# Latent attention by one written order of three engines, the next pair's expansions inside it, and o_B projected by token halves

## The chip, the cores and the metric

The kernel runs on one core of one Trainium2 chip. Its metric is the device time of one launch in microseconds (us). Four compute engines work beside each other: TensorE (PE) multiplies, VectorE (DVE) and ScalarE (ACT) work element by element, GpSimd (POOL) does small things and starts some transfers; SyncE (SP) starts the rest. The kernel lets PE write into eight banks of 512 columns of PSUM, which ACT and DVE read.

## What is computed

One encoder layer on 1024 prompt tokens and on 32 sample tokens with a past of 512. Two attention branches read one projection of the normalised input; the change is in branch A and in the projection of branch B's output.

```python
q = (rms_norm(q_lat, g_q_lat) @ w_uq).reshape(B, T, H_A, NOPE + ROPE)   # 8 heads, 64 + 32
k_nope, v_a = expand_latent(c_kv, w_uk, w_uv)                          # (c_kv @ w_uk), (c_kv @ w_uv)
s = (einsum('bqhd,bshd->bhqs', q_nope, k_nope)
     + einsum('bqhr,bsr->bhqs', q_rope, k_rope)) * MLA_SCALE
mask = (kpos[None, :] // CHUNK) <= (qpos[:, None] // CHUNK)            # CHUNK = 64
o_A = einsum('bhqs,bshd->bqhd', softmax(where(mask, s, NEG)), v_a)
merged = sigmoid(gate A) * (o_A @ w_proj_a) + sigmoid(gate B) * (o_B @ w_proj_b)
```

o_B comes from stick-breaking attention, which ran before. After `merged` come w_out, a residual, and a convolutional feed-forward block, none of them touched.

## The kernel before

A product is kept near fp32 by splitting each operand into a rounded high half and a low rest: `hi` (L60) is an ACT copy, `lo` (L63) a DVE subtraction, and `mm3` (L66) issues three products, high x high, high x low, low x high. Weights come through `wload` (L73; SP, two raw buffers "wr") and are split into "wh" and "wl", two buffers each.

The stages follow one another: `stage_h`, `stage_sb` (stick-breaking attention), `stage_lat` (latents), `stage_mla` (L1008), `stage_merge`, `stage_up`, `stage_down`. Within a stage a compile-time scheduler orders each engine's instructions by their priority and a cost model, except where a `manual_schedule` block holds: there PE, ACT and DVE keep the written order. `stage_sb` has such a block for each of its four head pairs: `ORDER` (L491) is a list of short words, `sb_attend` (L513) turns each into its instructions, and the words f, G, D, W, w call `gates` (L778), an independent projection whose products fill PE.

`stage_mla` before has none. For each of four head pairs p (L1020):
- it loads and splits w_uq and w_uk of the pair; `queries` (L1070) makes two heads' queries (18 mm3 of 352 columns, a multiplication by the rotary table on DVE at L1075, then hi and lo), `keys` (L1062) writes both heads' keys (4 mm3 of 512 columns) into the one pair of key buffers; for p 0 and 2 `values` (L1041) makes the values of four heads;
- for the sample, `mla_sample_expand` (L1174) makes keys and values of four heads from the cached latent, in column blocks of 272 and 272, (at p = 0 and 3), and `mla_sample` (L1197) attends (at p = 1 and 3);
- `attend` (L656) runs each head over u, the blocks of 256 query rows (0 to 3 for the first head, 3 to 0 for the second). For each of the 2 row tiles of 128 it makes scores (`score`, L1097: high x high, high x low, a mask product of 64 columns at L1104 for the diagonal, low x high) in one or two PSUM banks "s" (three of them), then `mla_weights` (L627): maximum on DVE (L633), exp with a row sum on ACT (L641), reciprocal on DVE, and the scaling on DVE (L651) or ACT (L653). Then pairs of 128-blocks are transposed on PE (L680) into a bank "tr" (two), split by hi and lo into PTh and PTl (or the two "ptd" tiles on the diagonal), and multiplied with the values (L693) into the one bank "pv", which is added up by ACT (L697) and DVE (L698);
- `proj_b` (L1233) projects one quarter of the tokens (264) of o_B: four loads and splits, then for each of 8 row tiles of w_proj_b a load, a split of 512 columns, 4 mm3, an ACT copy (L1250) and a store on POOL's queue. Its 384 products are independent of the attention, and the scheduler puts them where PE would wait.

After the four pairs the loop reads back the outputs of pairs 0 to 2, splits them and begins the products of w_proj_a with them (L1128 to 1146); the last pair's output is split directly.

Of the kernel before, what the change touches and what calls it, by code (L numbers as in the profile page):

```python
# [8 lines left out]
F32 = mybir.dt.float32  # L9
# [8 lines left out]
P = 128  # L18
D = 1024
KT = 8  # L20
# [17 lines left out]
UT = 1060  # L38


class K:
# [471 lines left out]
    def sb_attend(self, score, V, out, fill):  # L513
        nc = self.nc
        act, vec = nc.scalar.activation, nc.vector
        tiles, banks, seen, turned, pv, res = {}, {}, {}, {}, {}, {}
        for x in self.ORDER:
# [6 lines left out]
            if k in "SaelxckdE":  # L524
# [33 lines left out]
                continue  # L558
            n, jb = x[0], int(x[2:] or 0)
# [9 lines left out]
            elif k == "V":  # L569
                if jb == u:  # L570
                    pv[n] = self.bank("pv")
                self.values(h, u, jb, pv[n], V, turned.pop(x)[1:])
            else:
                r, q = slice(64 * h, 64 * h + 64), slice(64 - 64 * h, 128 - 64 * h)
                if k == "o":
                    res[n] = self.tl(self.At, [P, 256], F32, "o")
                    nc.scalar.copy(res[n][r], pv[n][q, :256])
                else:
                    vec.tensor_tensor(res[n][r], pv[n][r, :256], res[n][r], ALU.add)
                    out(res[n], r, slice(u * 256, u * 256 + 256))  # L580

# [44 lines left out]

    def mla_weights(self, pieces, w):  # L627
# [27 lines left out]

    def attend(self, h, score, weights, V, out, order=(0, 1, 2, 3)):  # L656

        nc = self.nc
        for u in order:
            at = []  # L660
            for i in (2 * u, 2 * u + 1):
                w = (i + 1) * P
                np_ = 1 if w <= 512 else 2
                n = w // np_
                pieces = []
                for j in reversed(range(np_)):
                    ps = self.tl(self.ps, [P, 512], F32, "s")
                    score(h, ps, i, j * n, max(n, 256), j == np_ - 1)
                    pieces.append((ps, j * n, n))
                at.append(weights(pieces, w))  # L670
            pv = self.bank("pv")
            for jb in range(2 * u, -1, -2):
                diag = jb == 2 * u
                tr = self.bank("tr")
                c0 = P if diag else 0
                for s in range(2):
                    b = jb + 1 - s
                    for q in range(2):
                        if b <= 2 * u + q:
                            nc.tensor.transpose(tr[:, (2 * s + q) * P : (2 * s + q + 1) * P],  # L680
                                                at[q][:, b * P : b * P + P], self.idt)
                if diag:
                    ph, pl = self.PTd[self.ptd_i % len(self.PTd)]
                    self.ptd_i += 1
                else:
                    ph = self.tl(self.At, [P, 512], F32R, "PTh")
                    pl = self.tl(self.At, [P, 512], F32R, "PTl")
                self.hi(ph[:, c0:], tr[:, c0:])
                self.lo(pl[:, c0:], tr[:, c0:], ph[:, c0:])
                for s in range(2):  # L690
                    b = jb + 1 - s
                    for j, x in enumerate((ph, pl)):
                        nc.tensor.matmul(pv[:, :256], V[:, b, h], x[:, s * 256 : s * 256 + 256],  # L693
                                         start=(diag and s == 0 and j == 0), stop=(jb == 0 and s == 1 and j == 1))
            o = self.tl(self.At, [P, 256], F32, "o")
            r, q = slice(64 * h, 64 * h + 64), slice(64 - 64 * h, 128 - 64 * h)
            nc.scalar.copy(o[r], pv[q, :256])  # L697
            nc.vector.tensor_tensor(o[r], pv[r, :256], o[r], ALU.add)  # L698
            out(o, r, slice(u * 256, u * 256 + 256))
# [198 lines left out]
    def stage_lat(self):  # L898
# [10 lines left out]
        self.QZm = L.tile([P, 4, 64], F32, name="QZm")  # L909
# [98 lines left out]
    def stage_mla(self):  # L1008
# [11 lines left out]
        for p in range(4):  # L1020
# [5 lines left out]
            h = self.tl(self.W, [P, 1024], F32R, "wh")  # L1026
            l = self.tl(self.W, [P, 1024], F32R, "wl")
            rq = raw[:, 0:576].rearrange("p (k h c) -> p k h c", k=3, h=2)
            hq, lq = (x[:, 0:768].rearrange("p (k h c) -> p k h c", k=3, h=2) for x in (h, l))
            for d0, s0, n in ((0, 0, 96), (96, 80, 16), (112, 64, 16)):  # L1030
                d, x = (slice(None),) * 3 + (slice(d0, d0 + n),), rq[:, :, :, s0 : s0 + n]
                self.hi(hq[d], x)
                self.lo(lq[d], x, hq[d])
            self.hi(h[:, 768:1024], raw[:, 576:832])
            self.lo(l[:, 768:1024], raw[:, 576:832], h[:, 768:1024])
            hk, lk = (x[:, 768:1024].rearrange("p (k c) -> p k c", k=2) for x in (h, l))
            KH, KL = ([x[(2 * p + e) % NK] for e in range(2)] for x in (KHs, KLs))
            gt = "mm" if p else "mm s s"
            QH, QL = [], []

            def values():  # L1041
                hf = p // 2
                raw = self.wload([(0, 512, a["w_uv"][0, :, hf * 256 : hf * 256 + 256]
                                   .rearrange("(k p) c -> p k c", p=P), 2)])
                h, l = self.wsplit(raw, 512)
                Vs = [self.tl(O, [P, 2 * T], F32R, "V")[:, : 16 * P].rearrange("r (t h d) -> r t h d", t=8, h=2)
                      for _ in range(2)]
                for t in range(0, 8, 2):
                    ps = self.bank(gt.split()[t // 2 % len(gt.split())])
                    for j in range(2):  # L1050
                        tk = slice((t + j) * P, (t + j + 1) * P)
                        for k in range(2):
                            self.mm3(ps[:, j * 256 : j * 256 + 256], self.CPh[k][:, tk], self.CPl[k][:, tk],
                                     h[:, k * 256 : k * 256 + 256], l[:, k * 256 : k * 256 + 256], k == 0, k == 1)
                    pv = ps.rearrange("r (j q h d) -> r j q h d", j=2, q=2, h=2)
                    for q in range(2):
                        self.hi(Vs[q][:, t : t + 2, :, 0:64], pv[:, :, q])
                        self.lo(Vs[q][:, t : t + 2, :, 64:128], pv[:, :, q], Vs[q][:, t : t + 2, :, 0:64])

                return Vs  # L1060

            def keys():  # L1062
                for c0, n, ps in self.mtile(hk, lk, self.CPh, self.CPl, ((0, 512), (512, 512)), 2, gt):
                    c = slice(c0, c0 + n)
                    for e in range(2):
                        r = slice(64 * e, 64 * e + 64)
                        self.hi(KH[e][0:64, c], ps[r, :n])
                        self.lo(KL[e][0:64, c], ps[r, :n], KH[e][0:64, c])

            def queries():  # L1070
# [998 lines left out]
```

## Time and profile before

| | |
|---|---|
| median of three runs | 1746.15 us (1742.15 to 1746.4) |
| the profiled execution | 1746.93 us, span 1745.2 us |
| granted TensorE clock, mean | 0.994 |
| ACT busy share of the span | 58% |
| HBM read and written | 174.25 MB and 51.25 MB |

A row of a timeline gives start, duration, engine, line, operation, output<-input and form. A row of a group gives line, engine, operation, output<-input, partitions x elements, the count, then busy time and mean ns of one, then the idle time before them and what ended it. "PE s L1105" is an instruction of PE that writes tile s at line 1105. PE's matmuls overlap in its pipeline and their ends are modelled. A stage's window starts at the first instruction named for it.

### The profile page before, as it was taken

How to read it: one execution, taken by the hardware profiler on the slowest of the kernel's cores; microseconds unless marked ns; L12 is line 12 of the kernel's file. 1: busy time of each engine (PE TensorE's matmuls, PEld its weight loads, DVE VectorE, ACT ScalarE, POOL GpSimd, SP SyncE). 2: the span in 40 equal slices, each digit the busy share in tenths (PEclk: the TensorE clock that was granted, in tenths of full speed). 3: DMA queues.
4: the chain of work that ended last, by engine and by line, in shares of the span. 5: the costliest groups of instructions: out<-in, count | busy, mean ns of one | idle time of the engine just before them, and what ended most of it. 6: DMA issues, size and time to landing. Idle time of an engine off the chain costs nothing. (4 is left out here: it accounts for less than half of the span.)

```text
span 1745.2 us, 29960 instructions
## 1 busy us (share of the span) xinstructions
PE 1701.0 (97%) x11546; PEld 1544.6 (89%) x11546; DVE 1259.0 (72%) x2133; ACT 1007.4 (58%) x1976; POOL 273.6 (16%) x519
## 2 busy tenths in 40 slices
PE   6999999999999999999999999999999999999998
PEld 3899999999989988888888779999999999977886
DVE  4596594693873678788686678887787787788456
ACT  4595594783872666867775267544444444544442
POOL 2211111111110001111000031212111111110013
PEclk8999999999999999999999999999999999999999
DMA  9343333333341222313346531434423323597743
GB/s 323 92 124 101 106 119 84 114 105 90 111 123 53 68 58 78 93 54 102 103 172 200 183 127 49 150 105 131 135 92 128 128 91 128 205 332 247 243 148 118
DMA packets 181695, 227.46 MB, mean 130 GB/s; under 512 B 13349, under 2 KB 129776, under 8 KB 181552
## 3 DMA queue, kind: packets, MB, share of 16 engines
q1 hardware_dynamic: 166048, 182.10, 33.2%
q0 software_dynamic: 15280, 43.35, 7.0%
q8 instruction: 91, 1.49, 0.3%
q14 instruction: 52, 0.43, 0.1%
q10 hardware_dynamic: 224, 0.09, 0.0%
HBM read 174.25 MB, written 51.25 MB: 129 GB/s over the span
## 5 line engine op out<-in xcount | busy, mean ns | idle before, releaser
L61 ACT ACTIVATE wh<-wr 128x1024 fp32r<-128x1024 f32 (+6 forms) x181 | 146.0, 813 | 259.4 <-PE s L1523 78.8
L64 DVE TENSOR_TENSOR wl<-wr,wh 128x1024 fp32r<-128x1024 f32 (+6 forms) x181 | 164.6, 916 | 145.3 <-ACT wh L61 141.9
L68 PE MATMUL mm<-hh,wh 128*128 128x352 f32 x696 | 232.1, 333 | 2.8 <-ACT nat L811 2.8
L69 PE MATMUL mm<-hl,wh 128*128 128x352 f32 x696 | 227.1, 326 | 0.3 <-DVE hl L288 0.3
L70 PE MATMUL mm<-hh,wl 128*128 128x352 f32 x696 | 226.0, 325 | 0.0
L68 PEld LDWEIGHTS mm<-hh,wh 128*128 128x128 f32 x696 | 131.5, 189 | 10.5 <-ACT nat L811 4.8
L69 PEld LDWEIGHTS mm<-hl,wh 128*128 128x128 f32 x696 | 131.5, 189 | 3.5 <-DVE hl L288 1.9
L70 PEld LDWEIGHTS mm<-hh,wl 128*128 128x128 f32 x696 | 131.6, 189 | 0.4 <-issue 0.4
L1524 PE MATMUL s<-T,wl 128*128 128x256 f32 (+1 forms) x328 | 93.6, 285 | 0.0
L1523 PE MATMUL s<-T,wh 128*128 128x256 f32 (+1 forms) x328 | 93.4, 285 | 0.0
L1522 PE MATMUL s<-T,wh 128*128 128x256 f32 (+1 forms) x328 | 93.3, 284 | 0.0
L1663 DVE SCALAR_TENSOR_TENSOR u<-u,c,u 128x1058 f32<-128x1058 f32 x68 | 87.0, 1317 | 2.0 <-ACT u L1660 0.7
L1522 PE MATMUL tr<-T,wh 128*128 128x272 f32 (+1 forms) x272 | 77.7, 286 | 0.0
L1524 PE MATMUL tr<-T,wl 128*128 128x272 f32 (+1 forms) x272 | 77.6, 285 | 0.0
L1523 PE MATMUL tr<-T,wh 128*128 128x272 f32 (+1 forms) x272 | 77.3, 284 | 0.0
L64 DVE TENSOR_TENSOR wl<-S,wh 128x1024 fp32r<-128x1024 f32 x40 | 48.9, 1223 | 34.8 <-ACT wh L61 34.8
L1524 PE MATMUL mm<-T,wl 128*128 128x256 f32 (+1 forms) x256 | 72.9, 286 | 0.3 <-DVE wl L64 0.2
L1522 PE MATMUL mm<-T,wh 128*128 128x256 f32 (+1 forms) x256 | 73.0, 285 | 0.0
L1523 PE MATMUL mm<-T,wh 128*128 128x272 f32 (+1 forms) x256 | 72.7, 284 | 0.0
L64 DVE TENSOR_TENSOR PTl<-tr,PTh 128x512 fp32r<-128x512 f32 x96 | 64.0, 683 | 8.5 <-ACT PTh L61 8.2
L1653 POOL COPY c<-u 128x2 f32<-128x2 f32 x44 | 26.7, 608 | 259.1 <-DVE u L1599 224.0
L61 ACT ACTIVATE wh<-S 128x1024 fp32r<-128x1024 f32 x40 | 42.4, 1060 | 35.0 <-PE s L1523 13.3
(674 smaller groups left out, 5618.9 us busy)
## 6 DMA issues: line engine op xcount, KB each, us to landing
wr<-in_w_ada_dram SPq DMA_DIRECT2D x48, 512.0 KB, 4.6
wr<-in_w_up_dram SPq DMA_DIRECT2D x44, 512.0 KB, 4.1
dr<-in_w_down_dram SPq DMA_DIRECT2D x43, 512.0 KB, 5.3
wr<-in_w_in_dram SPq DMA_DIRECT2D x33, 512.0 KB, 4.7
wr<-gdn SPq DMA_DIRECT2D x30, 512.0 KB, 4.9
gdn<-u POOLq DMA_DIRECT2D x23, 512.0 KB, 5.0
gd<-nat POOLq DMA_DIRECT2D x48, 176.0 KB, 2.2
t<-gd SPq DMA_DIRECT2D x16, 528.0 KB, 4.5
```

What stands on the lines that cost most here:

```text
L61: self.nc.scalar.activation(out, in_, AF.Identity, scale=scale)
L64: return self.nc.vector.tensor_tensor(out, full, hi.bitcast(F32), ALU.subtract)
L68: m(ps, lh, rh, start=start, stop=False)
L69: m(ps, lh, rl, start=False, stop=False)
L70: self.pe = m(ps, ll, rh, start=False, stop=stop).ins
L1522: m(ps[:, :n], w[0][:, k], x[0][:, k, c], start=first and k == 0, stop=False, skip_group_check=True)
L1523: m(ps[:, :n], w[0][:, k], x[1][:, k, c], start=False, stop=False, skip_group_check=True)
L1524: i = m(ps[:, :n], w[1][:, k], x[0][:, k, c], start=False, stop=k == 3, skip_group_check=True)
L1653: nc.gpsimd.tensor_copy(self.CV[:, 0:2, cc], u[:, 1024:1026])
L1663: nc.vector.scalar_tensor_tensor(y, u[:, w : w + YW], self.cvT[:, w, cc : cc + 1], y, ALU.mult, ALU.add)
```

## The change

`attend` goes. Two written orders come, ORDER_A for pairs 0 to 2 and ORDER_L for the last, and `mla_attend` turns their words into instructions inside a `manual_schedule` block, as `sb_attend` does. The words T, h, v, V, o, p (transposes, hi, lo, products with values, sums) are now one function, `sums`, for both attentions. Attention's words are S scores, M maximum, m its join over two banks, E exp, s sum's join, R reciprocal, C scaling on DVE, c on ACT.

The other words fill:
- f, G, U, W, w, O are `proj_b`: one mm3, a store, a load, a high half, a low half, the operands. It now goes by halves of the tokens (528), each in two column blocks of 264, and w_proj_b's eight row tiles come in six loads of one or two.
- I, i, x, X, y, H, L, z, J, j, Z are the next pair's expansion: split of its weights, queries of head 0 (x), keys (y), queries of head 1 (z), and their evictions. They are in ORDER_A only; pair 0's own run ahead of the loop.
- Y is a step of the sample's second attention, q and r the split of an output; these are in ORDER_L only.

Between the blocks, without a written order: for p = 1 `mla_sample_keys` and the sample's first expansion, for p = 2 the keys again, the values of heads 4 to 7, the sample's first attention, the second expansion, and o_B's second operands. The sample's cached and new latents are kept in separate tiles, so its expansions have column blocks of 512 and 32. The wh and wl buffers are taken once as the two sets AB, shared by all of this. The second head's rotary key rows are copied from the first's by two POOL transfers in place of a second split.

```diff
+PARTS = ((0, 0, 96), (96, 80, 16), (112, 64, 16))
...
+    ORDER_A = """
+        S0.0 S0.1 S1.0 W f M0.0 f M0.1 M1.0 f E0.0 f E0.1 w f E1.0 S1.1 G R0.0 R0.1 R1.0 c0.0 S2.0a C0.1 c1.0
+        M1.1 S2.0b M2.0a T0.0 E1.1 f M2.0b h0.0 f R1.1 m2.0 C1.1 E2.0a f v0.0 E2.0b S2.1a G s2.0 S2.1b R2.0
...
+        T4.2 X c5.0 S5.1b h4.3 S6.0 h4.2 M5.1b x v4.3 x v4.2 T4.1 m5.1 M6.0 E5.1a V4.3 h4.1 V4.2 E5.1b x v4.1
+        E6.0 T4.0 s5.1 X f R5.1 R6.0 W V4.1 C5.1 S6.1 G w h4.0 T5.2 c6.0 v4.0 S7.0 h5.2 x M6.1 T5.1 v5.2 E6.1
+        V4.0 M7.0 h5.1 x R6.1 C6.1 o4 T5.0 v5.1 E7.0 x h5.0 p4 S7.1 R7.0 X c7.0 y v5.0 J V5.2 M7.1 V5.1 Z E7.1 j
+        V5.0 T6.1 o5 T6.0 h6.1 R7.1 p5 y C7.1 h6.0 v6.1 z v6.0 H z H L V6.1 V6.0 L T7.0 o6 z h7.0 p6 z X z v7.0
+        z y X V7.0 y o7 p7 z H z H L z L X Z J j
+    """.split()
+
+    ORDER_L = """
+        S0.0 S0.1 S1.0 W f M0.0 f M0.1 M1.0 f E0.0 f E0.1 w S1.1 E1.0 G S2.0a R0.0 R0.1 R1.0 c0.0 M1.1 c1.0
...
+        h3.3 s4.0 R4.0 h3.2 v3.3 c4.0 f v3.2 T3.1 Y f h3.1 S4.1a G v3.1 V3.3 M4.1a V3.2 V3.1 T3.0 S4.1b h3.0
+        S5.0a v3.0 f M4.1b f V3.0 M5.0a f m4.1 o3 f E4.1a p3 G q S5.0b E4.1b r M5.0b S5.1a s4.1 m5.0 R4.1 E5.0a
+        C4.1 E5.0b S5.1b M5.1a T4.3 s5.0 M5.1b T4.2 h4.3 R5.0 S6.0 m5.1 c5.0 v4.3 h4.2 M6.0 T4.1 E5.1a V4.3 v4.2
+        h4.1 E5.1b V4.2 v4.1 E6.0 T4.0 s5.1 R5.1 V4.1 R6.0 C5.1 h4.0 S6.1 c6.0 v4.0 T5.2 M6.1 T5.1 h5.2 V4.0
+        E6.1 v5.2 S7.0 o4 T5.0 R6.1 h5.1 M7.0 p4 S7.1 h5.0 C6.1 V5.2 v5.1 q E7.0 v5.0 T6.1 V5.1 r h6.1 V5.0 R7.0
+        M7.1 c7.0 v6.1 T6.0 E7.1 o5 R7.1 h6.0 C7.1 p5 v6.0 q V6.1 r V6.0 T7.0 o6 h7.0 p6 v7.0 q r V7.0 o7 p7 q r
+    """.split()
...
+        AB = [[self.tl(self.W, [P, 1024], F32R, g) for g in ("wh", "wl")] for _ in range(2)]
...
+        proj = self.proj_b(M, AB)
+        steps, QH, QL = expansion(0, "mm s s")
+        raw = load_values(0)
+        steps["I"]()
+        steps["i"]()
+        for _ in range(2):
+            for k in "yyHHLL":
+                steps[k]()
+        Vs = values(0, raw, "mm s s")
+        proj["O"]()
+
+        self.hi(KHs[0][64:128], self.KRp[64:128])
+        self.lo(KLs[0][64:128], self.KRp[64:128], KHs[0][64:128])
+        for x in (KHs, KLs):
+            nc.gpsimd.dma_start(x[1][64:128], x[0][64:128])
+        for k in "xxxXxxxXxxxXJjZ":
+            steps[k]()
+        for k in "zzzXzzzXzzzXJjZ":
+            steps[k]()
+        for k in "UUWwU":
+            proj[k]()
+
+        for p in range(4):
+            if p == 1:
+                expanded = self.mla_sample_expand(M, raw, AB[1], *self.mla_sample_keys(M))
+            if p == 2:
+                cn = self.mla_sample_keys(M)
+                Vs = values(1, raw, "mm")
+                for _ in self.mla_sample(0, QZ, QR, *expanded):
+                    pass
+                proj["U"]()
+                expanded = self.mla_sample_expand(M, raw_s, AB[1], *cn)
+                proj["O"]()
+            if p in (1, 2):
+                for k in "UWwU":
+                    proj[k]()
...
+            with self.tc.manual_schedule(engines={E.PE, E.Activation, E.DVE}):
+                self.mla_attend(self.ORDER_L if p == 3 else self.ORDER_A, score, Vs[p % 2], out, fill)
...
+    def proj_b(self, M, AB):
...
+        HB = HC // 2
+        TILES = ((0, 1), (1, 2), (3, 1), (4, 1), (5, 2), (7, 1))
...
+        def operands():
+            h = done[0] // 6
+            ob[:] = [self.tl(M, [P, 4, HC], F32R, g) for g in ("ObH", "ObL")]
+            for k in range(4):
+                f = self.tl(self.At, [P, BIG], F32, "big")[:, :HC]
+                nc.sync.dma_start(f, self.obd[k][:, h * HC : h * HC + HC])
+                self.hi(ob[0][:, k], f)
+                self.lo(ob[1][:, k], f, ob[0][:, k])
```

446 lines of the change are left out of this document (277 added, 169 removed).

## Prediction

> **What bounds the kernel now.** I read the page's totals first.
>
> ```profile
> span 1745.2 us, 29960 instructions
> PE 1701.0 (97%) x11546; PEld 1544.6 (89%) x11546; DVE 1259.0 (72%) x2133; ACT 1007.4 (58%) x1976; POOL 273.6 (16%) x519
> ```
>
> TensorE is the bound, and by this row nearly without a gap, so a new order could win little. But the ends of matmuls are modelled: one that waits inside the array's pipeline still counts as busy. So I next read starts, in the timeline of PE, in fed stretches:
>
> ```profile
> 644.25 0.28 PE L70 MATMUL mm<-ObH,wl 128*128 128x264 f32 x1
> 644.37 0.28 PE L68 MATMUL mm<-ObH,wh 128*128 128x264 f32 x1
> 644.68 0.47 PE L1100 MATMUL s<-KH,QH 128*128 128x448 f32 x1
> ...
> 645.39 0.40 PE L1100 MATMUL s<-KH,QH 128*128 128x512 f32 x1
> 645.62 0.39 PE L1101 MATMUL s<-KL,QH 128*128 128x512 f32 x1
> 645.86 0.20 PE L1104 MATMUL s<-c,c 128*128 128x64 bf16 x1
> 645.89 0.48 PE L1105 MATMUL s<-KH,QL 128*128 128x512 f32 x1
> ...
> 881.99 0.32 PE L68 MATMUL mm<-KH,wh 128*128 128x352 f32 x1
> 882.15 0.32 PE L69 MATMUL mm<-KL,wh 128*128 128x352 f32 x1
> 882.30 0.32 PE L70 MATMUL mm<-KH,wl 128*128 128x352 f32 x1
> 883.40 0.50 PE L1100 MATMUL s<-KH,QH 128*128 128x512 f32 x1 [0.78 <-ACT A L641]
> ...
> 885.80 0.98 PE L680 MATMUL tr<-c,A 128*128 128x128 f32 x7 [0.35 <-DVE A L651]
> 886.54 0.41 PE L68 MATMUL mm<-QH,wh 128*128 128x352 f32 x1
> ```
>
> Fed, a product of 264 columns takes 0.12 us from start to start, one of 352 0.16, one of 512 0.235, a mask product 0.03, and seven transposes 0.74, so 0.106 each. Between 264 and 512 that is 0.455 ns a column. Two rows show stalls. The score at 644.68 comes 0.31 after a product that takes 0.12: 0.19 us lost and no idle time shown. The score at 883.40 comes 1.10 after one that takes 0.16; of the 0.94 lost, the row shows 0.78 and names the exp (L641) that held its bank.
>
> Now the stage that the change rewrites, from its first product (604.2) to the first product with the last pair's output (897.6), beside a stretch of the stick-breaking stage, which a written order drives already:
>
> ```profile
> 205.00:265.00 60.00, 59.28 (x419) 54.78 (x418) 57.72 (x103) 54.31 (x121) 8.54 (x16) 1.00 0.39 120
> 604.20:897.60 293.40, 285.06 (x1949) 252.68 (x1950) 230.62 (x563) 217.32 (x537) 33.95 (x59) 1.00 0.28 87
> ```
>
> (Columns: length; busy time and count of PE, weight loads, DVE, ACT, POOL; granted clock; DMA share; GB/s.) The groups by line price PE's own work in the 293.4 us; mm3 issues three products a call, so one row of three is shown:
>
> ```profile
> L680 PE MATMUL tr<-c,A 128*128 128x128 f32 x288 | 42.4, 274 | 0.8 <-DVE A L651 0.8
> L69 PE MATMUL mm<-ObL,wh 128*128 128x264 f32 (+1 forms) x144 | 41.6, 290 | 0.5 <-DVE ObL L64 0.5
> L1100 PE MATMUL s<-KH,QH 128*128 128x384 f32 (+4 forms) x96 | 36.6, 384 | 2.2 <-ACT A L641 1.7
> L693 PE MATMUL pv<-PTh,V 128*128 128x256 f32 x96 | 27.6, 292 | 0.0
> L693 PE MATMUL pv<-ptd,V 128*128 128x256 f32 x128 | 26.6, 299 | 1.5 <-DVE o L698 0.9 <-ACT ptd L61 0.3
> L68 PE MATMUL mm<-lat,wh 128*128 128x352 f32 (+1 forms) x74 | 25.2, 340 | 0.0
> L1104 PE MATMUL s<-c,c 128*128 128x64 bf16 x64 | 13.0, 203 | 0.0
> L68 PE MATMUL mm<-wh,lat 128*128 128x256 f32 x24 | 7.2, 300 | 0.6 <-DVE KL L64 0.6
> ```
>
> 432 x 0.12 = 51.8; 288 x 0.106 = 30.5; the scores of one head have 256+256+384+512+640+768+896+1024 = 4736 columns, so 8 heads x 3 products x 4736 x 0.455 ns = 51.7; values against transposed weights 320 (128, 96 and 96 again for the low half) x 0.12 = 38.4; queries 180 x 0.16 and keys 42 x 0.235 = 38.7; masks 64 x 0.03 = 1.9; values of the latent 72 x 0.12 = 8.6; the remaining 263, of 64 to 352 columns, at 0.14 = 36.8. Sum 258.4. So **35 us of the 293.4 are stalls of PE**, though the row shows 8.3 idle. That is all the change can win; everything else is outside it.
>
> **The change part by part.**
>
> *o_B by halves.* Products and evictions stay at 384 and 32. Weight splits fall from 32 of 512 columns to 8 of 512 and 4 of 1024:
>
> ```profile
> L64 DVE TENSOR_TENSOR wl<-wr,wh 128x512 fp32r<-128x512 f32 x34 | 23.0, 683 | 3.9 <-ACT wh L61 3.0 <-PE tr L713 0.8
> L64 DVE TENSOR_TENSOR wl<-wr,wh 128x1024 fp32r<-128x1024 f32 x2 | 2.4, 1216 | 0.0
> L61 ACT ACTIVATE wh<-wr 128x512 fp32r<-128x512 f32 x34 | 21.6, 637 | 10.2 <-PE mm L69 9.3 <-ACT KH L61 0.9
> L61 ACT ACTIVATE wh<-wr 128x1024 fp32r<-128x1024 f32 x2 | 2.1, 1058 | 0.0
> ```
>
> and the page's row of loads (KB each, us to landing):
>
> ```profile
> wr<-in_w_in_dram SPq DMA_DIRECT2D x33, 512.0 KB, 4.7
> ```
>
> DVE 21.9 to 10.3, ACT 20.4 to 9.3, and 4.2 MB of weights less on SP. All of it lies beside PE's work: nothing on the path now, but it leaves room on DVE and ACT. Without it DVE would be some 3 us a pair fuller, and where DVE is the later one in a block, that much would be late. Only two raw weight buffers exist, and each SP load waits for the low half of the one before; a load is issued at a low half and used a third of a block (some 15 us) later, lands in 4.7, and DMA is 0.28 busy: so at nothing. If one came late, the split behind it on ACT would wait up to those 4.7, with transposes' evictions queued behind it. The second half's operands sit in one buffer: the first half's 64 steps end inside block 1, so its refill waits for nothing. K's rotary rows for the second head go by two POOL transfers in place of two splits: beside PE, nothing.
>
> *Written order.* Attention's own instructions per pair stay: 24 score groups, 20 transpose groups, 20 value groups. What goes is the scheduler's order. A written block for pairs 0 to 2 holds on PE: attention 51.7/4 + 30.5/4 + 38.4/4 + 1.9/4 = 30.6, 32 steps of o_B (96 x 0.12 = 11.5), 18 query steps (54 x 0.16 = 8.6) and 4 key steps (12 x 0.235 = 2.8): 53.5 us. The last pair's holds 30.6 + 11.5 + some 3 of the sample's = 45. Over four blocks 206. Can DVE and ACT keep up? They are busy 230.6 and 217.3 us in this stage, some 53 and 50 a quarter even with the work outside the blocks, against 53.5 of PE there, and both get lighter, as shown. The nearest row is the stick-breaking stretch: DVE 57.72 and ACT 54.31 of 60. Counted by the same prices (these rows),
>
> ```profile
> L68 PE MATMUL mm<-hh,wh 128*128 128x352 f32 x69 | 23.1, 335 | 0.7 <-ACT nat L811 0.7
> L589 PE MATMUL tr<-c,A 128*128 128x128 f32 x57 | 8.2, 275 | 0.0
> L473 PE MATMUL s<-KH,Q 128*128 128x512 f32 (+4 forms) x21 | 7.5, 359 | 0.0
> L603 PE MATMUL pv<-PTh,V 128*128 128x256 f32 x18 | 4.6, 282 | 0.0
> L200 PE MATMUL mm<-wr,cT 128*32 128x256 f32 x48 | 3.4, 387 | 0.0
> ```
>
> PE's work there is 208 x 0.16 + 57 x 0.106 + 42 x 0.16 + 64 x 0.12 + 3.4 (the 48 of L200, their busy time) = 57.1 of 60. So under a written order with DVE 96% busy PE loses at most 5%, where the scheduled stage loses 12%. Bounds for the four blocks: 0 (nothing stalls) to 5% of 206, 10. I take 7, nearer the upper end, since the last pair has no expansions to fill with and its last o_B step stands two thirds into the order.
>
> A strict order also adds waits. On ACT an exp that waits for its maximum has the eviction of transposes (PTh) queued behind it, and PE waits for those; on DVE a maximum that waits for its score has the low halves behind it. The stretch's row says that this cost PE at most those 5%. The Trainium skill, "TensorE: Matmul & The Clock Gate", section "Architectural detail: the array is 16× 32×32, not 1× 128×128", states that ACT and DVE are strict FIFO, while PE can pull weight loads ahead: so one badly placed wait in the two lists is not repaired at run time. By the row the sum is 7; were that rule to bite at each score tile, it is the slower rival below.
>
> *Expansions moved inside, sample's products between.* The queries and keys of the next pair become filler; their work is counted above. Between blocks 0 and 1 the sample's expansion stands alone, between 1 and 2 its second keys, the values, the first sample attention and the second expansion. Each first needs a split by ACT and DVE behind the block's last ones. Bounds for each gap on PE: below nothing (the next block's three first scores run ahead) and 3.5 (a split of 1024 columns, 1.06 + 1.22, then one of 512 of a transpose, as the rows above price them). Nearest is the wait between the stick-breaking pairs:
>
> ```profile
> 288.02 0.33 PE L69 MATMUL mm<-hl,wh 128*128 128x352 f32 x1
> 288.79 0.66 PE L710 MATMUL tr<-c,A 128*128 128x128 f32 x4 [0.44 <-ACT A L624]
> ...
> 290.12 1.10 PE L724 MATMUL pv<-A,big 128*128 128x64 f32 x8
> 291.15 0.32 PE L724 MATMUL pv<-A,vsb 32*128 32x64 f32 x1
> ```
>
> 0.61 lost at 288.79, with other products to run; here there are fewer. I take 2.5 each, 5. Between blocks 2 and 3 nothing stands.
>
> *Sample keys in 512 + 32 columns in place of 272 + 272.* 24 such couples. Before about 2 x 0.125. After 0.235 plus a 32-column product that the trace does not show: between 0 and the 0.13 of 64-column ones (8 in 1.03). So -0.4 to +2.8; I take 2.8, whose row is nearest.
>
> *Ends.* The opening has waits for its first splits, of which this is the first:
>
> ```profile
> 604.25 0.51 PE L68 MATMUL s<-wh,lat 128*128 128x256 f32 x2 [0.56 <-ACT wh L61]
> ```
>
> It keeps them, some 2 in all. At the end the last u-blocks of head 1 are a chain; the products of w_proj_a with finished pairs fill it, as they do at 882: 2.
>
> **Sum** for the profiled execution, which ran 1746.9 us for a span of 1745.2: 35 of stalls go; 7 + 5 + 2 + 2 = 16 come back, and 2.8 of work: gain 35 - 16 - 2.8 = 16. That gives 1731; the median shown, 1746.15, lies 0.8 below that execution. **I forecast 1731**, its own range 1724 to 1740 (blocks 0 to 10, gaps 0 to 7, the 32-column term, some 4 us for rounding in the 258).
>
> **Rivals.**
> - *All stalls go.* The stick-breaking stretch at zero, gaps filled by the next block's scores: 4 come back at the ends, and 2.8 of work: gain 28, so 1719. For it: the stretch's missing 5% may be my prices. Against: the last pair lacks filler.
> - *The wait is only moved.* The order holds, but the gaps cost their 3.5 each, the blocks 5%, the last chain 8, and DVE or ACT come late once a pair by 2: 7 + 10 + 8 + 8, nearly all the 35 with the 2.8. About 1746, so no change; this is also what comes out if the written order is no better than the scheduler's. Against: the stretch.
> - *Slower: the head of a strict list.* Place: the score tiles. Their exp frees the bank; if PE's list always reaches the score before that, each pays what 883.40 paid (0.78 shown). 64 tiles x 0.78 = 50, and 2.8 of work: 18 over the 35, so 1765. It decides from about 41 tiles of 64 ((35 - 2.8) / 0.78). Against: 16 tiles a pair with three score banks is what stick-breaking has, under longer chains of ACT.
>
> **How the numbers follow.** Forecast 0.58, all stalls go 0.17, only moved 0.13, slower 0.12. The range leaves out the slower case, the top of the third and the bottom of the second: 1718 to 1745. A measurement of this kernel tells about 0.3% (5 us) from no change: faster by more than that has the first two, 0.75; within it 0.13; slower 0.12.
>
> **What would show it.** Right: PE's count of products in the stage stays near 1949, the stage is some 277 us long, starts inside the blocks come at the fed spacings, DVE is 90% or more busy there, and what waits remain lie between blocks 0 and 1, 1 and 2, and in the last third of the last pair. Wrong: scores that start late behind L641's successor in every pair; a wait for a weight load; a gap over 4 us between blocks; or a later stage that moves by more than 2 us, which none of these steps touches.

## The result, and the profile after

The changed kernel takes 1734.92 us (median of six runs, 1733.42 to 1736.54), the kernel before 1745.31 beside it (six runs, 1742.15 to 1748.04). The ratio is 0.9941, with a 95% interval of 0.9930 to 0.9951: 10.4 us or 0.6% faster. The forecast was 1731.

The profiled execution of the changed kernel ran 1733.42 us for a span of 1731.7. The totals of its page:

```profile
PE 1691.4 (98%) x11546; PEld 1540.8 (89%) x11546; DVE 1249.7 (72%) x2104; ACT 994.5 (57%) x1943; POOL 274.6 (16%) x521
```

The products are as many as before. The share of PE rose by one point, and says nothing about where 10 us went. So again the stage itself, from its first own product to the first product with the last pair's output, and under it the four blocks from first score to first score (columns as in the prediction: length; busy time and count of PE, weight loads, DVE, ACT, POOL; granted clock; DMA share; GB/s):

```profile
602.04:887.80 285.76, 280.07 (x1951) 251.14 (x1950) 220.86 (x534) 205.41 (x506) 34.50 (x61) 1.00 0.24 76
621.92:680.66 58.74, 58.05 (x412) 52.72 (x411) 46.94 (x117) 43.34 (x106) 9.19 (x16) 1.00 0.24 72
680.66:751.12 70.46, 69.34 (x481) 61.39 (x479) 53.85 (x127) 50.86 (x125) 9.15 (x16) 1.00 0.22 68
751.12:824.94 73.82, 73.59 (x530) 67.70 (x529) 52.22 (x134) 50.01 (x129) 10.21 (x18) 1.00 0.21 64
824.94:887.80 62.86, 60.65 (x419) 52.23 (x419) 49.89 (x123) 47.44 (x117) 4.88 (x9) 1.00 0.28 101
```

The stage went from 293.40 to 285.76: 7.6 us. A second profile of the changed kernel gives 285.39, so this stage's length repeated within 0.4 us; the kernel before has one profile only. The other 2.4 to 2.8 of the 10.4 us lie outside these bounds, and the record doesn't show whether they are the change's. The granted clock scatters what lies there: the stage starts at 603.3 to 604.6 us in the seven profiles whose first 60 us ran at a granted clock of 0.89, the kernel before among them, and at 601.1 to 602.7 in the seven with 0.91 to 0.94. What lies behind the stage takes 847.6 us before, 843.9 and 846.3 in the two profiles of the changed kernel, and up to 850 in other runs of this study.

DVE is busy 80, 76, 71 and 79% of the four blocks, not the 90% that the prediction expected. Over the stage DVE does 9.8 us less than before and ACT 11.9, as the halves promised.

Which waits are left? PE's waits in the stage (who, for whom; us in total, times, longest):

```profile
PE mm L72 <- DVE KL L68: 1.4, 1, 1.4
PE s L1208 <- ACT A L711: 1.4, 4, 0.7
PE tr L603 <- DVE PTl L68: 0.8, 2, 0.4
PE tr L603 <- DVE A L718: 0.6, 1, 0.6
PE pv L617 <- DVE ptd L68: 0.4, 2, 0.2
```

With one more of 0.2 only 4.8 us in all, where the same list of the kernel before adds up to 7.6; the first row is the opening. But starts tell more than waits, as the prediction found. Priced by the median spacing of each form (the sample's score products of 272 columns at 0.14), the 1949 products of the stage need about 259.0 us before and 261.2 after (the 32-column products); over it stand about 34.3 before and 24.6 after. By blocks the 24.6 are 2.4 in the opening, 3.7, 6.0 and 3.8 in the three blocks with expansions, and 8.6 in the last pair's.

Two kinds of this remainder are no waits for another engine. One is the product behind a mask. PE's timeline after, around one of them:

```profile
630.86 0.37 PE L1208 MATMUL s<-KH,QH 128*128 128x448 f32 x1
631.07 0.36 PE L1209 MATMUL s<-KL,QH 128*128 128x448 f32 x1
631.27 0.20 PE L1212 MATMUL s<-c,c 128*128 128x64 bf16 x1
631.31 0.45 PE L1213 MATMUL s<-KH,QL 128*128 128x448 f32 x1
631.60 0.82 PE L603 MATMUL tr<-c,A 128*128 128x128 f32 x6
```

The first two products of 448 columns take 0.21 and 0.20, the mask 0.04, and the product behind it 0.29: 0.08 to 0.09 more. That holds for all five lengths and in both kernels, so a mask costs 0.12, where the prediction gave it 0.03: 64 x 0.09 = 6 us. The other are some 16 of the sample's plain score products of 272 columns at about 0.3 each in place of 0.14, 3 us.

### The profile page after: what moved, and what is told of

The parts are those of the page before. It is cut to its first block, busy times and chain, and to the rows that moved or that the text cites. A ratio compares the mean times of both kernels' runs of the same rounds, so it can differ in the third digit from the quotient of the medians.

```text
span 1731.7 us, 29842 instructions
## 1 busy us (share of the span) xinstructions
PE 1691.4 (98%) x11546; PEld 1540.8 (89%) x11546; DVE 1249.7 (72%) x2104; ACT 994.5 (57%) x1943; POOL 274.6 (16%) x521
## 5 line engine op out<-in xcount | busy, mean ns | idle before, releaser
L65 ACT ACTIVATE wh<-wr 128x1024 fp32r<-128x1024 f32 (+6 forms) x161 | 134.3, 844 | 252.1 <-PE s L1737 80.0
L68 DVE TENSOR_TENSOR wl<-wr,wh 128x1024 fp32r<-128x1024 f32 (+6 forms) x161 | 154.4, 967 | 148.0 <-ACT wh L65 147.7
L603 PE MATMUL tr<-c,A 128*128 128x128 f32 x576 | 83.4, 275 | 1.5 <-DVE PTl L68 0.8
L68 DVE TENSOR_TENSOR PTl<-tr,PTh 128x512 fp32r<-128x512 f32 x100 | 67.2, 683 | 11.9 <-ACT PTh L65 11.4
L603 PEld LDWEIGHTS tr<-c,A 128*128 128x128 f32 x576 | 66.4, 140 | 9.6 <-DVE PTl L68 1.7
```

The costliest lines, as they stand in the source:

```text
L65: self.nc.scalar.activation(out, in_, AF.Identity, scale=scale)
L68: return self.nc.vector.tensor_tensor(out, full, hi.bitcast(F32), ALU.subtract)
L603: self.nc.tensor.transpose(tr[:, (2 * s + q) * P : (2 * s + q + 1) * P], at[q][:, b * P : b * P + P], self.idt)
```

## The experiments

**The theories.** Theory 1: these 9 us are work, and the rest of the gain came as forecast, by the order. Theory 2: everything over the spacings is waiting, set by the order and by VectorE and ScalarE. All times below are medians against the kernel before on the same chip, with the ratio and its 95% interval; "the stage" is bounded as above.

### The changed kernel again

No edit.

> The changed kernel once more, as it is, for the noise of the parts that the change doesn't touch and as the base of the runs beside it. Both theories: 1733 to 1737 us and the latent attention's own stretch (from its first own product to the first product of the merge that follows) at 285 to 287 us, against 293 of the kernel before; if the stretches before and behind it differ again by up to 2 us each from the kernel before, that part of the gain is not the change's.

1733.68 us; 0.9945 (0.9930 to 0.9960). Stage 285.39.

### Without the masks, in both kernels

```diff
-                if last:
-                    d = i * P - c0 + 64
-                    m(ps[:, d : d + 64], self.idb, self.mk64, start=False, stop=False)
```

> The changed kernel without the 64 mask products of the latent attention's scores (so the causal mask of that part is left out). Theory 1 (about 9 of the 35 us that the prediction counted as stalls are TensorE's own work, most of it the product behind each mask, which starts .083 us later than its neighbours because its weights are not loaded beside so short a stream): a mask costs .04 + .083 = .122 us, so 64 of them 7.8 us; the stretch goes from about 286 to 278 and the time from about 1735 to 1727. Theory 2 (what is left over the products' spacing are waits by the three engines' strict order, paced by VectorE and ScalarE): the 64 masks are worth at most the 64 x .03 to .04 = 2 to 2.5 us that the prediction gave them and part of that turns into waiting, so 1733 to 1735.

> The kernel before, without the same 64 mask products (the same part of the computation left out). Theory 1: the masks are the same work in both kernels, so 6 to 8 us less than the kernel before (about 1738 where it is 1745). Theory 2: 0 to 2.5 us less (1743 to 1745), since there the waits are longer still and take in what the masks leave.

The changed kernel: 1733.10; 0.9931 (0.9914 to 0.9947). The kernel before: 1746.36; 1.0008 (0.9999 to 1.0018). The stage without masks, of the changed kernel and of the kernel before:

```profile
601.69:885.04 283.35, 275.84 (x1886) 251.57 (x1886) 220.45 (x534) 205.31 (x506) 34.61 (x61) 1.00 0.24 76
```

```profile
602.70:898.67 295.97, 283.11 (x1885) 255.46 (x1886) 230.86 (x563) 217.79 (x536) 32.80 (x59) 0.98 0.28 86
```

The second row can't be read as it stands, for its granted clock is 0.98. From 757.5 to 760.9 and from 873.5 to 880.4 this execution ran at half clock (0.50 and 0.51): the 44 products that start there took 9.8 us, where their median spacings add up to 5.3. Less these 4.5 us the stage is some 291.5 us long, 1.9 less than with the masks; this is an estimate. The times are no better: the ten runs without masks had a median clock of 0.9935, the kernel before beside them 0.996.

The product behind the place of the mask did lose its 0.08, as the same stretch of PE's timeline without masks shows (0.21, 0.19, 0.21):

```profile
630.46 0.36 PE L1208 MATMUL s<-KH,QH 128*128 128x448 f32 x1
630.67 0.36 PE L1209 MATMUL s<-KL,QH 128*128 128x448 f32 x1
630.86 0.37 PE L1210 MATMUL s<-KH,QL 128*128 128x448 f32 x1
631.07 0.93 PE L603 MATMUL tr<-c,A 128*128 128x128 f32 x7
```

So PE's work fell by 7.8 us, and the stage by 2.0 to 2.4 after and, by the estimate, by some 2 before (under a schedule that the scheduler made anew). Theory 1 falls in its second half: work taken from PE came back as waits. So the 24.6 us over the spacings can't be divided once for all into work and stall.

### The mask on 128 columns, and the mask twice

```diff
+        self.mk128 = ct([P, P], BF16)
+        nc.vector.memset(self.mk128, 0.0)
+        nc.vector.memset(self.mk128[0:64, 64:128], NEG)
...
-                    m(ps[:, d : d + 64], self.idb, self.mk64, start=False, stop=False)
+                    m(ps[:, d - 64 : d + 64], self.idb, self.mk128, start=False, stop=False)
```

> The changed kernel with each mask product streaming 128 columns (64 of zeros ahead of the 64 that mask), so .03 us more of stream each by the spacing of the transposes' 128 columns. Theory 1 (an exposed weight load): the load of the next product's weights has so much more to hide behind, its late start shrinks by as much, from .083 to about .05, and the time is the same as the changed kernel's within 1 us. Rival to it (a fixed price of going from bf16 to the other type): the late start stays at .083 and 64 x .03 = 1.9 us come on top.

1737.22; 0.9958 (0.9943 to 0.9973); stage 285.49. The stage lies between those of the changed kernel's two profiles, 285.39 and 285.76; its median time is 3.5 higher than that of the changed kernel beside it, 1733.68, and nothing in the stage shows why. The follower's late start stays at 0.08, against theory 1's weight load; but the 64 columns more cost nothing, against the rival. The trace doesn't tell where the 0.12 come from, only that 64 columns cost as much as 128.

For the next runs the question was which engine has slack: theory P says that TensorE (PE) sets the pace of the blocks, theory V that VectorE and ScalarE do. The same mask product is now issued twice:

```diff
                     m(ps[:, d : d + 64], self.idb, self.mk64, start=False, stop=False)
+                    m(ps[:, d : d + 64], self.idb, self.mk64, start=False, stop=False)
```

> The changed kernel with each mask product issued twice (the sum of two masks masks as one does). Taking the 64 masks away gave about 2 us where 7.8 of TensorE's time went with them, so theory 1 as it stood is wrong in that point; two readings are left. Theory P (TensorE paces the blocks, and the written order is fitted to its pace, so that time taken from it is only waited for elsewhere): a second mask costs its full .12 us, 64 x .122 = 7 to 8 us more, so about 1742. Theory V (VectorE and ScalarE pace the blocks, and TensorE has slack that its spacing doesn't show): half of it or less, 0 to 4 us more.

1736.58; 0.9958 (0.9943 to 0.9972); stage 286.02, 0.3 to 0.6 longer. The number is theory V's, but the premise was wrong. PE's timeline:

```profile
633.80 0.20 PE L1212 MATMUL s<-c,c 128*128 128x64 bf16 x1
633.84 0.19 PE L1213 MATMUL s<-c,c 128*128 128x64 bf16 x1
633.87 0.46 PE L1214 MATMUL s<-KH,QL 128*128 128x448 f32 x1
634.16 0.60 PE L603 MATMUL tr<-c,A 128*128 128x128 f32 x4
```

The second mask takes 0.03, and the late start of the product behind (0.29) is paid once. PE got 64 x 0.03 = 1.9 us of work, of which 0.3 to 0.6 show. That speaks for slack on TensorE, as the runs without masks do, but weakly.

### o_B's weight splits twice

```diff
             self.hi(w[-1][0], raw[0][:, :n])
+            self.hi(w[-1][0], raw[0][:, :n])
...
             self.lo(w[-1][1], x[:, : w[-1][1].shape[-1]], w[-1][0])
+            self.lo(w[-1][1], x[:, : w[-1][1].shape[-1]], w[-1][0])
```

> The changed kernel with each weight split of o_B done twice (the same values written again), which puts 12 more instructions of 512 and 1024 columns on each of VectorE and ScalarE, about 10 and 9 us, as much as the halves had taken off. Prediction and theory P: they lie in the idle 25% of VectorE and 28% of ScalarE, 0 to 2 us more. Theory V: they are on the path, 5 to 10 us more.

1743.88; 0.9999 (0.9989 to 1.0010): the whole gain is gone. The stage, and the three largest of PE's waits in it:

```profile
603.33:896.76 293.43, 282.17 (x1950) 251.67 (x1950) 230.62 (x546) 214.28 (x518) 34.51 (x61) 1.00 0.24 74
```

```profile
PE tr L603 <- DVE A L718: 3.1, 2, 1.6
PE pv L617 <- DVE ptd L68: 2.4, 6, 0.7
PE tr L603 <- DVE PTl L68: 1.6, 3, 0.8
```

DVE grew by 9.8 us, ACT by 8.9 and the stage by 7.7 to 8.0, though DVE stands idle a fifth of the time. All of PE's listed waits come to 10.1 us, 5.3 more than without the second splits. One of these places, at the head of the first block, in the timeline of all engines:

```profile
627.36 1.22 DVE L68 TENSOR_TENSOR wl<-wr,wh 128x1024 fp32r<-128x1024 f32 x1
...
628.63 1.22 DVE L68 TENSOR_TENSOR wl<-wr,wh 128x1024 fp32r<-128x1024 f32 x1
...
629.76 0.28 DVE L716 RECIPROCAL sum<-sum 128x1 f32<-128x1 f32 x3
629.95 0.91 ACT L720 ACTIVATE A<-A,sum 128x128 f32<-128x128 f32 x2 [1.53 <-DVE sum L716]
...
630.42 0.55 PE L603 MATMUL tr<-c,A 128*128 128x128 f32 x3 [1.51 <-DVE A L718]
```

The second split is one instruction of 1.22 us. Behind it in DVE's list stand three reciprocals of 0.1 each; ACT's scaling waits 1.53 for them, and the transposes 1.51. That is theory V, by place: the list is late at one point, though the engine isn't full. The run doubles the splits on both engines; what each of them costs was not taken apart.

### The strict order taken away

```diff
-            with self.tc.manual_schedule(engines={E.PE, E.Activation, E.DVE}):
+            with ExitStack():
```

> The changed kernel's steps in the same written sequence, but with the order on the three engines left to the scheduler (the three engines' strict order taken away, nothing else). Prediction: the order is what takes the short waits out of the blocks, so some 7 us of the stage's gain go, 1739 to 1743. Rival: the sequence in which the steps are issued, with the expansions in it, carries the gain already, and the time stays within 2 us of the changed kernel's.

1730.95 (1729.29 to 1737.22); 0.9935 (0.9912 to 0.9959). The forecast of this run was wrong: nothing is lost. The stage is even 2.5 to 2.9 us shorter, and so are PE's waits in it:

```profile
601.08:883.97 282.89, 279.55 (x1951) 251.79 (x1950) 219.88 (x534) 206.20 (x506) 33.50 (x61) 1.00 0.24 76
```

```profile
PE mm L72 <- DVE KL L68: 1.4, 1, 1.4
PE s L1208 <- ACT A L711: 0.5, 3, 0.2
```

With three more of 0.2 each 2.5 us in all; the waits for PTl and for ptd are gone, and so is that for A of L718. Whether this version is faster than the changed kernel the times don't settle; the intervals overlap.

### The expansions behind the block, with and without the strict order

```diff
-                self.mla_attend(self.ORDER_L if p == 3 else self.ORDER_A, score, Vs[p % 2], out, fill)
+                self.mla_attend(self.ORDER_L if p == 3 else
+                                [x for x in self.ORDER_A if x[0] not in "xyzXJjZHL"], score, Vs[p % 2], out, fill)
+            for k in "xxxXxxxXxxxXJjZyyHHLLyyHHLLzzzXzzzXzzzXJjZ" if p < 3 else "":
+                steps[k]()
```

> The changed kernel with the products of the next pair's expansion, and what reads them, behind the block instead of in its last third (the weight's split stays where it is). Prediction: the gaps between blocks come back, 2 x 2.5 us, and the blocks lose what fills their ends, 2 to 7 us more: 7 to 12 us in all, 1741 to 1746. Rival (o_B's products alone fill a block): the gaps alone, 4 to 6 us, about 1739.

> The changed kernel with neither the strict order nor the expansions inside the blocks: the scheduler orders the written sequence, and the next pair's products stand behind the block. Each of the two alone gave within 3 us of the changed kernel. Theory V: what is left is the halves, 1734 to 1738. If either of the two is enough by itself (they stand in for each other): 1740 to 1745.

With the strict order 1735.90; 0.9954 (0.9939 to 0.9969); stage 285.18. Without it 1734.14; 0.9934 (0.9916 to 0.9952); stage 285.35. The stage gets no longer by it: the losses expected of the first run, 4 to 12 us, were wrong. The second came in at the number that theory V had; its reason, that the halves are what is left, is tested next. Strict order and expansions inside, taken away together, cost nothing of the stage's gain. With the expansions behind the block the strict order costs nothing either, 285.18 against 285.35.

### The halves of o_B alone, in the kernel before

```diff
...
-                if p == 3:
-                    expanded = self.mla_sample_expand(1, M)
+            if p == 2:
+                expanded = self.mla_sample_expand(1, M)
...
-        NQ = T // 4
...
+        hf, tiles = i // 2, (((0, 1), (1, 2), (3, 1)), ((4, 1), (5, 2), (7, 1)))[i % 2]
+        if i % 2 == 0:
+            self.ob = [self.tl(M, [P, 4, HC], F32R, g) for g in ("ObH", "ObL")]
...
+        for m0, nm in tiles:
...
```

> The kernel before with one part of the change alone: o_B by token halves (12 weight splits in the place of 32, the three blocks of six tiles spread over the pairs as they come, products behind each pair's attention as before, scheduler's order; the sample's second expansion moves one pair earlier, since it shared o_B's operand tile). The split work that goes is that which costs 9 us when it is put back into the changed kernel. Theory V (the short splits on VectorE and ScalarE were on the path, so the halves carry the gain): 7 to 9 us less than the kernel before, about 1736. Theory P and the prediction (the halves are hidden, the order and the expansions inside carry the gain): within 2 us of the kernel before. A third reading (the doubled splits hurt only because the written order leaves them no other place): 0 to 4 us less.

1744.72; 0.9995 (0.9984 to 1.0006), so between 2.8 us less and 1.0 more. The stage, and inside it a stretch at half clock with two of its products:

```profile
602.65:897.50 294.85, 286.30 (x1949) 253.96 (x1950) 222.35 (x535) 207.93 (x508) 32.64 (x59) 0.99 0.24 73
881.10:887.90 6.80, 6.28 (x24) 5.39 (x25) 4.38 (x11) 4.64 (x12) 0.00 (x0) 0.50 0.01 2
```

```profile
883.31 0.41 PE L1100 MATMUL s<-KH,QH 128*128 128x256 f32 x1
883.52 0.42 PE L1101 MATMUL s<-KL,QH 128*128 128x256 f32 x1
```

At a granted clock of 0.50 these two products of 256 columns start 0.21 us apart, where 0.12 is the median; the 24 products that start in the stretch took 6.4 us in place of 3.1. Less these 3.3 us, an estimate, the stage is some 291.5 us long, 1.9 less than that of the kernel before. DVE's load fell from 230.62 to 222.35 us and ACT's from 217.32 to 207.93, and the stage by 2 at most. So theory V holds for the place of a split, and its 7 to 9 us are out: the halves by themselves bring little. Between nothing and the 0 to 4 us of the third reading these numbers don't decide.

### o_B's steps behind the block too

```diff
+            order = self.ORDER_L if p == 3 else self.ORDER_A
...
+                self.mla_attend([x for x in order if x[0] not in "xyzXJjZHLfGWwIi"], score, Vs[p % 2], out, fill)
+            for x in order:
+                if x[0] in "fGWwIi":
+                    for _ in range(int(x[1:] or 1)):
+                        fill(x[0])
+            for k in "xxxXxxxXxxxXJjZyyHHLLyyHHLLzzzXzzzXzzzXJjZ" if p < 3 else "":
+                steps[k]()
```

> The kernel without strict order and without expansions inside (1734), and now with all of o_B's steps (its products, weight splits and evictions) and the expansion's weight split behind each block's attention in the written sequence too, as the kernel before has them; what is left of the written sequence is the attention's own (scores, maxima, exponentials, transposes and values of several tiles staggered), and the scheduler may draw the rest forward by itself. Theory F (the gain is o_B's products written between the attention's steps): back to the kernel before, 1741 to 1746. Theory A (the gain is the staggered sequence of the attention's steps): 1732 to 1737. The prediction's share, 7 us in the blocks and 5 between them, would be a mixture, about 1740.

1741.53; 0.9973 (0.9964 to 0.9983), between the two theories and near the mixture. Stage, and beside it that of the kernel with neither the strict order nor the expansions inside, which differs by o_B's steps alone (and the split of the expansion's weights):

```profile
603.81:893.84 290.03, 284.01 (x1951) 253.21 (x1951) 222.84 (x536) 208.01 (x507) 34.80 (x61) 1.00 0.24 75
```

```profile
602.03:887.38 285.35, 281.60 (x1951) 251.84 (x1951) 220.86 (x534) 206.64 (x506) 33.82 (x61) 1.00 0.24 76
```

So 4.7 us of the stage hang on o_B's steps standing between the attention's in the sequence that the scheduler is given. By the times it is 6.6 (gains of 4.2 and 10.8), and some of that lies behind the stage: there the first 600 products take 104.2 us with o_B's steps behind the blocks and 101.7 without. The 3.4 from 293.4 to 290.0 belong to what this kernel keeps of the change: the staggered sequence of the attention's steps, the order of the work between blocks, the sample's other column blocks, the halves (2 at most, alone). These I didn't take apart.

### o_B's low halves on GpSimd

```diff
-            self.lo(w[-1][1], x[:, : w[-1][1].shape[-1]], w[-1][0])
+            self.nc.gpsimd.tensor_tensor(w[-1][1], x[:, : w[-1][1].shape[-1]], w[-1][0].bitcast(F32), ALU.subtract)
```

(without the strict order)

> The changed kernel's sequence in the scheduler's order (1731 before) with the low half of o_B's weight splits on GpSimd, which is busy 12% of the stage: 12 instructions, 10.3 us, leave VectorE. Theory V: VectorE is part of the pace, 2 to 6 us less, 1725 to 1729. Theory P: nothing, 1730 to 1732; if GpSimd is so slow that the low parts come late, slower than 1732.

1738.07; 0.9956 (0.9939 to 0.9973); stage 287.46, where it was 282.89 with these parts on VectorE. Slower, and not only because GpSimd is slow. Its groups in the stage, and the timeline of all engines at one of them:

```profile
L1443 POOL TENSOR_TENSOR wl<-wr,wh 128x512 fp32r<-128x512 f32 x8 | 10.7, 1334 | 15.8 <-ACT wh L65 15.7
L1443 POOL TENSOR_TENSOR wl<-wr,wh 128x1024 fp32r<-128x1024 f32 x4 | 9.5, 2386 | 8.8 <-ACT wh L65 8.7
```

```profile
633.04 0.15 DVE L714 TENSOR_TENSOR sum<-sum 128x1 f32<-128x1 f32 x1
...
633.86 1.51 DVE L709 TENSOR_TENSOR mx<-mx 128x1 f32<-128x1 f32 x1
...
634.04 1.30 POOL L1443 TENSOR_TENSOR wl<-wr,wh 128x512 fp32r<-128x512 f32 x1
...
636.12 0.47 PE L1208 MATMUL s<-KH,QH 128*128 128x448 f32 x1 [0.55 <-ACT A L711]
```

A DVE instruction on one column, 0.15 us elsewhere, took 1.51 and ended just behind GpSimd's subtraction; the exp behind it waited, and the score behind that exp. Four of the 32 joins of maxima (L709) did so, at 1.1 to 1.5 us each, each beside a subtraction of 512 columns. They are not alone: nine DVE instructions of the stage, all between tiles in SBUF (copies and a scaling among them), each beside one of the 12 subtractions, took together 10.2 us more than their medians without the edit. That is as much as had left DVE, whose load rose from 219.88 to 222.11 us. How much of the 4.6 us these stops cost, and how much the late low halves, was not taken apart.

## Why the prediction was right, and what in it was not

**Direction and size.** Right: 10.4 us of gain where 16 were forecast, inside the forecast's own range of 1724 to 1740. What the stage itself shows is 7.6 to 8.0, half of the forecast: it is 285.4 to 285.8 us long, not some 277. By the stage alone the time would be about 1738, still inside the range, but 7 us off. That the time came out nearer to 1731 is luck as far as the record shows, since no step of the prediction touches what lies outside the stage. One of its own signs of being wrong, a later stage that moves by more than 2 us, can't be judged: what lies behind moved by 1.3 in one profile and by 3.7 in the other, and in the second the granted clock from 1000 to 1030 us was 1.00, where it was 0.94 before.

**The 35 us of stalls.** The count holds (34.3 by median spacings). But some 7 to 9 us of it are no waits for another engine (masks and the sample's plain products), and the changed kernel keeps them. Without the masks some 5.6 of their 7.8 us came back as waits: they lay beside other limits.

**What comes back, 16.** This is the term that was mis-sized: 24.6 came back. (The 2.8 of added work came out at 2.2, the 32-column products at 0.11 us each.) By its parts: the opening 2.4 (2 forecast). The first three blocks with the gaps behind them 13.5, masks included (the forecast's 12 for blocks and gaps held the last pair's block too); the next block's first scores do run ahead, as its lower bound had it, so the gap between blocks 0 and 1 is short, and that between 1 and 2 is mostly the sample's slow products. The last pair 8.6, where the forecast had 2 for its end and a share of the 7. Two of its waits, in the timeline after:

```profile
829.55 1.22 DVE L68 TENSOR_TENSOR wl<-wr,wh 128x1024 fp32r<-128x1024 f32 x1
...
831.87 0.55 PE L603 MATMUL tr<-c,A 128*128 128x128 f32 x3 [0.58 <-DVE A L718]
```

```profile
863.46 1.09 ACT L65 ACTIVATE KH<-big 128x1056 fp32r<-128x1056 f32 x1 [1.32 <-DMA big<-oa]
...
864.97 0.69 ACT L711 ACTIVATE A<-s,mx 128x512 f32<-128x512 f32 x1
...
865.80 0.41 PE L1208 MATMUL s<-KH,QH 128*128 128x320 f32 x1 [0.67 <-ACT A L711]
```

The first is the pattern of the doubled splits, once, by o_B's own split. The second is a split from behind the block, of the outputs read back: it waited 1.32 us for its DMA at the head of ACT's list, with the exp queued behind it.

**The rule on strict lists.** The Trainium skill, "TensorE: Matmul & The Clock Gate", section "Architectural detail: the array is 16× 32×32, not 1× 128×128", was weighed with nothing of its own in the sum. These rows agree with it: what stands behind a long or waiting instruction on ACT or DVE is late. The slower rival had the right kind of wait and the wrong place and number: it put one at each of 64 score tiles, and PE's list shows four late scores, 1.4 us together, and a few late transposes and products with values. Two of these stand in the last thirds of blocks 0 and 1, here the first:

```profile
663.35 1.23 DVE L68 TENSOR_TENSOR wl<-wr,wh 128x1024 fp32r<-128x1024 f32 x1 [0.44 <-ACT wh L65]
...
664.49 0.68 DVE L68 TENSOR_TENSOR PTl<-tr,PTh 128x512 fp32r<-128x512 f32 x1
...
664.60 0.32 PE L74 MATMUL mm<-lat,wl 128*128 128x352 f32 x1
...
665.32 0.63 PE L603 MATMUL tr<-c,A 128*128 128x128 f32 x4 [0.40 <-DVE PTl L68]
```

The transposes start 0.72 behind a product that takes 0.16. The split ahead of PTl belongs to the sample's expansion between the blocks: the prediction had it "behind the block's last ones", and the scheduler drew it forward into the block.

**The written order and the expansions inside.** Here the cause was wrong. The prediction gave the gain to the strict order and to the expansions as filler. Stage lengths by what each kernel has (one profile each, the changed kernel two):

| kernel | o_B halves | staggered sequence, other order between blocks | o_B among the steps | expansions inside | strict | stage, us |
|---|---|---|---|---|---|---|
| before | | | | | | 293.4 |
| halves alone | x | | | | | 294.9 (some 291.5 less its half clock) |
| o_B behind | x | x | | | | 290.0 |
| neither | x | x | x | | | 285.4 |
| expansions behind | x | x | x | | x | 285.2 |
| not strict | x | x | x | x | | 282.9 |
| changed | x | x | x | x | x | 285.4, 285.8 |

The gain is in the sequence: 3.4 us by its staggering and what came with it (the halves are up to 2 of these), 4.7 by o_B among the steps. The expansions inside give 2.5 more where the scheduler may place them; there the strict order takes 2.5 to 2.9 back, and with the expansions behind the block nothing. So the condition of the second rival came true, for the written order is no better than the scheduler's, and its time, 1746, did not: what the prediction overlooked is the sequence that the scheduler is given.

**The halves at nothing.** Nearly right: alone they bring 2 us of the stage at most, and 0.9995 by time. The price named for losing that room, about 3 us a pair, came out at 2 (7.7 to 8.0 us over four pairs, and that with ACT's splits doubled too). Not tried: whether the doubled splits would cost as much without the strict order.

**DVE at 90%.** Wrong, 71 to 80%. The prediction's quarters were off as well: its row of 230.6 and 217.3 us gives 57.7 and 54.3 a quarter, not 53 and 50, so by its own row DVE and ACT were fuller than PE's 53.5; but much of that load lies outside the blocks, which hold 46.9 to 53.9 of DVE each. The comparison with the stick-breaking stretch, where DVE is 96% busy, therefore bounded something else. DVE and ACT aren't full here, and the doubled splits, the masks and the halves together speak for this reading: the place of an instruction in the chain of a tile through three engines decides, not an engine's load.

## What to carry to other kernels

Before a gain is put down to a strict order, run the same written sequence under the scheduler: here the sequence carried the gain, and the strictness cost up to 2.9 us or nothing. Before a stage's length is compared with another's, look at the granted clock in both rows: two of the lengths here were 3 to 5 us too long by it. In a list that ACT or DVE must follow, look for the long weight split that stands just ahead of a one-column step of the chain, and try to split it or move it behind (not tried here); an engine that is idle a fifth of the time is no cover for it. And time taken from a 98% busy TensorE is worth only what the chain through the other engines lets through.

## What the runs showed of the hardware

- A mask product of 64 bf16 columns costs 0.12 us with its follower's late start (0.04 + 0.08), and one of 128 columns the same. A second mask right behind the first costs 0.03.
- GpSimd's subtraction takes 1.33 us for 512 columns and 2.39 for 1024, where VectorE takes 0.68 and 1.22, and while one runs a VectorE instruction between tiles in SBUF can stand still until it ends (1.51 us for 0.15; nine such instructions beside 12 subtractions). The Trainium skill, "SBUF — State Buffer", section "SBUF: two separate sides", calls the port pair of these two an exclusive lock, held for a whole instruction; the rows above agree, though the VectorE instruction's record starts 0.18 us before GpSimd's.
- At a granted clock of 0.50 products of 256 columns start 0.21 us apart, at 1.00 they start 0.12 apart. Such stretches of 3.4 and 6.8 us stand in the stage in two of the 14 profiles, three in all; each begins beside a wait of PE of 0.9 to 2.6 us, and what sets them off is not shown.
